# Layer 2's modulation computed as row sums on VectorE, and a longer gap between layer 1's gate matmuls and their transposes

## The chip, the cores and the metric

The kernel runs as one program on one core of a Trainium2 chip. The metric is the device time of one execution in microseconds (us). The engines are TensorE (PE in the profile; its weight loads are PEld), VectorE (DVE), ScalarE (ACT), GpSimd (POOL) and SyncE (SP), on whose queue all data transfers of this kernel are issued. Each engine works through its own instructions in order.

## The reference

A trunk of two layers over 512 tokens of width 1024 plus 256 context tokens. Per layer, shortened:

```python
shift, scale, gate = split(silu(c) @ ada_w + ada_b, 3)      # c: one vector of 1024; ada_w: 1024 x 3072
hx = rms_norm(x, norm_w) * (1 + scale) + shift              # the same for the context y, with c_ctx
... = split_cols(hx @ w_in)                                 # q, k, v, gates of three branches, merge gates
ret, na, gqa = retention(...), neighbourhood_attention(...), grouped_query_attention(...)
m = sum(sigmoid(mg_b) * (branch_b @ w_b_o) for the three branches)
x = x + gate * (m @ w_out)                                  # the same for y, in layer 1 only
return rms_norm(x, final_norm_w)                            # after layer 2
```

The change concerns the first line alone: `shift`, `scale` and `gate`, called the modulation here. For each layer it is a product of a 3072 x 1024 matrix with one vector (x) or two (x and context). Layer 1 is `l == 0` in the code, layer 2 is `l == 1`.

## The kernel before

Activations lie with features on the 128 partitions and tokens along the free dimension (8 tiles of 128 features; 768 columns in layer 1, 512 in layer 2's queries and outputs). Every large product is made of three matmuls (lines 286 to 288): weights are split into `whi` (cast by ScalarE, L270) and `wlo` (the remainder, by GpSimd or VectorE, L272), activations likewise. Weights come as a stream of 512 KB tiles `raw`, two buffers deep, issued on SP's queue in the order of use; `whi` and `wlo` have five half-tile buffers each.

The order of TensorE's instructions is the order in which the code is written (a manual schedule). On the other engines a scheduler places instructions by a simulated time and by priorities.

At the end of each layer stands `finish` (L1261), the end stage, in two parts:

- Eight merge units, one per feature tile d (`u_merge`, L1085): 24 matmuls of 512 columns and, in layer 1, 24 of 256 for the merge gate, then 12 and 12 for the retention branch's output projection. ScalarE takes the gate's PSUM bank through a tanh into the tile `mt`; VectorE multiplies the projection's bank into `mt` (L1114) and adds it to the sum `m[d]` (L1115). Then `m[d]` is split into a high part by ScalarE (L1278) and a low part by VectorE (L1279), in tiles `mhl` for d below 4 and `gat` above.
- The output projection `g_out` (L1289): two passes over the token columns (512 and 256 in layer 1, 256 and 256 in layer 2), eight tiles each, each a sum over all eight split tiles, that of d = 7 last. VectorE evicts a bank with the gate `cG` and the old x (`xo`) (L1302), ScalarE squares, VectorE sums the squares (L383). The norm of the first pass is computed under the second.

The modulation stands in slices of 256 of the 3072 columns (`ada_slice`, L345). A slice is a 1 MB transfer into `araw`; eight matmuls (L352) that write four groups of 32 PSUM rows; a copy of the bank by VectorE into `aev` (L355); two transposes by TensorE (L360), placed some microseconds of TensorE's work later by `defer`; and a few small VectorE instructions (L365 to L371) that leave `adaT`, `cA` (from the scale) and `cG` (from the gate). Layer 1's first eight slices run at the kernel's start. The other sixteen run in layer 1's end stage: two after each merge unit d = 0 to 3 (layer 1's four gate slices after d = 0 and 1, layer 2's shift and scale after that), one after each of d = 4 to 7, and layer 2's four gate slices in the first pass of `g_out`. After d = 7, `due(True)` forces the transposes of that slice at once.

Of the kernel before, what the change touches and what calls it, by code (L numbers as in the profile page):

```python
# [8 lines left out]
F32 = mybir.dt.float32  # L9
# [4 lines left out]
ALU = mybir.AluOpType  # L14
# [3 lines left out]
DEPTH = 2  # L18
# [18 lines left out]


@with_exitstack
def trunk_kernel(ctx: ExitStack, tc: tile.TileContext, xt, wcol, wv, adaw, wbr, wout, nabias, vecs,  # L40
                 cst, cst16, out, taps=None):
    nc = tc.nc

    def tap(name, ap, where):
# [205 lines left out]
    NKEEP = ((0.01, 0.01, 0.01, 0.0), (5.0, 0.01, 4.0, 0.0))  # L250
    GAP = 2.0
    XA0 = 5
    SN0 = 5
    LEAD = 1.5
    stream = []
# [81 lines left out]
    ap_wout = [[[wout[l, t] for t in range(8)] for _ in range(2)] for l in range(DEPTH)]  # L337


    def ada_load(l, s, apool, bufs):  # L340
        raw = apool.tile([128, KT, 256], F32, tag="araw", name="araw", bufs=bufs)
        nc.sync.dma_start(out=raw, in_=adaw[l, s].rearrange("p (k c) -> p k c", c=256))
        return raw

    def ada_slice(l, s, apool, bufs, raw=None):  # L345
# [739 lines left out]
    def u_merge(l, b, d, g, m, getpool):  # L1085
        gq = G_ALL if l == 0 else G_LAT
        nq = NT if l == 0 else NX
        src = [ap_wcol[l][CT_MG + 8 * b + d]]
        if d % 2 == 0:
            src.append(ap_wbr[l][b][d // 2])  # L1090

        def gen(ws):
            if d % 2 == 0:
                wbr_now[0] = ws[1]
            t = getpool().tile([128, nq], F32, tag="mt", name="mt", bufs=1)

            def ev(ps, o, n):
                nc.scalar.activation(t[:, o:o + n], ps, AF.Tanh, scale=0.5)
            yield from g_proj(ws[0], gq, ev)
            hi, lo = wbr_now[0][d % 2]  # L1100
            if len(g) < 4:
                due(True)
            for o, n in gq:
                ps = pbank()
                for k in range(4):
                    c = slice(k * 128, k * 128 + 128)
                    gh, gl = g[k]
                    mm3(ps[:, :n], hi[:, c], lo[:, c], gh[:, o:o + n], gl[:, o:o + n], k == 0, k == 3)
                    if k == 3:
                        c = slice(o, o + n)  # L1110
                        if b == BR_NA:
                            nc.vector.scalar_tensor_tensor(m[d][:, c], t[:, c], 1.0, ps[:, :n], op0=ALU.add, op1=ALU.mult)
                        else:
                            nc.vector.scalar_tensor_tensor(t[:, c], t[:, c], 1.0, ps[:, :n], op0=ALU.add, op1=ALU.mult)  # L1114
                            nc.vector.tensor_tensor(m[d][:, c], m[d][:, c], t[:, c], op=ALU.add)  # L1115
                    yield 3 * n * NS
        return Unit(nq * 36 * NS, src, gen)

# [142 lines left out]
    def finish(l, m, mtp):  # L1261
        nq = NT if l == 0 else NX
        cm = pool(f"wo{l}")
        op = cm.__enter__()
        mp = env["mp"]
        mhl = {}
        for d, u in enumerate(end_units[l]):
            run([u], True)
            if l == 0:
# [19 lines left out]
        def g_out(half, o, n):  # L1289
            for d in range(KT):  # L1290
                w = getw(ap_wout[l][half][d])
                xo = op.tile([128, 512], F32, tag="xo", name="xo", bufs=2)
                nc.sync.dma_start(out=xo[:, :n], in_=xsrc[:, d * st + o:d * st + o + n])
                ps = pbank()
                for k in range(KT):
# [3 lines left out]
                    if k == KT - 1:  # L1299
                        s = 1 if o >= NX else 0  # L1300
                        with tc.high_priority(HP):
                            nc.vector.scalar_tensor_tensor(xn[d][:, o:o + n], ps[:, :n], cG[l][:, d, s:s + 1], xo[:, :n],  # L1302
                                                           op0=ALU.mult, op1=ALU.add)
                            sumsq(accs["t"], xn[d], d == 0, slice(o, o + n), op)
                        if l == 0 and o == 0:
                            nc.sync.dma_start(out=env["xsave"][:, d * NX:(d + 1) * NX], in_=xn[d][:, :NX])
                        tap(f"x{l}", xn[d][:, o:o + n], (d, slice(None), slice(o, o + n)))
# [128 lines left out]
def _layout(x, c, ctx, c_ctx, ada_w, ada_b, norm_w, w_in, ret_log_decay, ret_gn_w, na_rpb,  # L1436
# [12 lines left out]
    a["adaw"] = aw[:, :, :, order].reshape(DEPTH, KT, 128, 12, 256).transpose(0, 3, 2, 1, 4).reshape(DEPTH, 12, 128, 2048)  # L1449
# [18 lines left out]
    return a  # L1468


_INS = ["xt", "wcol", "wv", "adaw", "wbr", "wout", "nabias", "vecs", "cst", "cst16"]


# [19 lines left out]
```

## Time and profile before

| | |
|---|---|
| median of 3 runs | 1732.67 us (1730.77 to 1734.23) |
| profiled execution, own time | 1732.19 us |
| its span, first to last instruction | 1730.4 us |
| mean granted TensorE clock | 0.993 |
| PE busy | 1660.4 us (96%) |
| DVE, ACT, POOL busy | 61%, 46%, 32% |
| layer 1's end stage | about 799 to 1000 us |
| layer 2's end stage | about 1590 us to the end |

Times in the trace are microseconds from the start of the span. A row of the timeline gives start, length, engine, line, operation, output and inputs, and in brackets how long the engine had been idle and what ended it. A row of a window gives its length, each engine's busy time with its instructions, the granted clock, the transfers' share and GB/s. Matmuls overlap in the records, so the distance between two starts, and not the length, is what a matmul costs.

### The profile page before, as it was taken

To read this page: it belongs to the slowest core of one execution; us is meant where nothing else is said; L and a number is where in the kernel's file an instruction comes from. 1 tells how busy PE (TensorE), PEld (TensorE's weight loads), DVE (VectorE), ACT (ScalarE), POOL (GpSimd) and SP (SyncE) were. 2 spreads that over 40 slices of the span, in tenths; PEclk is the share of its full clock that TensorE was granted. 3 is DMA by queue.
4 is the path that set the end of the run, shared out by engine and by line. 5 is a ranking of instruction groups with operands and counts; after the bars stand their busy time and mean duration, and the time that the engine had idled before them with its cause. 6 is when DMAs were issued, how large, how long until landed. Compare 5 with 4: busy or idle time off the path is not lost. (4 is left out here: it accounts for less than half of the span.)

```text
span 1730.4 us, 26113 instructions
## 1 busy us (share of the span) xinstructions
PE 1660.4 (96%) x9940; PEld 1438.0 (83%) x9940; DVE 1058.3 (61%) x2201; ACT 797.0 (46%) x1570; POOL 555.5 (32%) x486
## 2 busy tenths in 40 slices
PE   5999999999999999999999999999999999999996
PEld 4878888888899889888887889877787898888786
DVE  6666567666655665565324766668777646556456
ACT  4455564555553443443223445654555534444342
POOL 1423332332332222322222343433333333243432
PEclk9999999999999999999999999999999999999998
DMA  8211111111111111214536521311111222222344
GB/s 319 86 46 56 58 46 53 37 49 37 37 50 59 50 58 40 62 49 155 211 134 207 171 94 51 99 51 62 49 49 51 71 63 72 61 78 69 104 139 148
DMA packets 43053, 146.38 MB, mean 85 GB/s; under 512 B 4912, under 2 KB 10160, under 8 KB 39856
## 3 DMA queue, kind: packets, MB, share of 16 engines
q1 hardware_dynamic: 42928, 144.72, 25.2%
q8 instruction: 78, 1.28, 0.3%
q14 instruction: 47, 0.39, 0.1%
HBM read 140.51 MB, written 4.19 MB: 84 GB/s over the span
## 5 line engine op out<-in xcount | busy, mean ns | idle before, releaser
L272 POOL TENSOR_TENSOR wlo<-raw,whi 128x512 fp32r<-128x512 f32 x345 | 456.3, 1328 | 959.3 <-ACT whi L270 904.8
L286 PE MATMUL pj<-hxh,whi 128*128 128x512 f32 (+1 forms) x1192 | 429.4, 360 | 1.2 <-DVE mt L1114 1.0
L287 PE MATMUL pj<-hxl,whi 128*128 128x512 f32 (+1 forms) x1192 | 414.3, 348 | 0.0
L288 PE MATMUL pj<-hxh,wlo 128*128 128x512 f32 (+1 forms) x1192 | 414.2, 348 | 0.0
L270 ACT CAST whi<-raw 128x512 fp32r<-128x512 f32 x376 | 231.1, 618 | 282.1 <-PE pj L287 169.9
L288 PEld LDWEIGHTS pj<-hxh,wlo 128*128 128x128 f32 x1192 | 225.3, 189 | 30.4
L286 PEld LDWEIGHTS pj<-hxh,whi 128*128 128x128 f32 x1192 | 225.7, 189 | 20.3 <-DVE mt L1114 1.4
L287 PEld LDWEIGHTS pj<-hxl,whi 128*128 128x128 f32 x1192 | 226.2, 190 | 18.3
L447 DVE TENSOR_TENSOR pl<-pt,ph 128x512 fp32r<-128x512 f32 (+2 forms) x208 | 126.8, 626 | 53.9 <-ACT ph L446 51.9
L446 ACT CAST ph<-pt 128x512 fp32r<-128x512 f32 (+2 forms) x208 | 107.6, 533 | 70.5 <-PE pt L632 30.6
L286 PE MATMUL pj<-gat,whi 128*128 128x512 f32 (+1 forms) x320 | 112.2, 351 | 2.0 <-ACT gat L925 2.0
L287 PE MATMUL pj<-gat,whi 128*128 128x512 f32 (+1 forms) x320 | 110.2, 344 | 0.2 <-DVE gat L926 0.2
L288 PE MATMUL pj<-gat,wlo 128*128 128x512 f32 (+1 forms) x320 | 110.1, 344 | 0.0
L286 PE MATMUL pt<-hxh,whi 128*128 128x512 f32 (+1 forms) x256 | 96.3, 376 | 1.0 <-ACT hxh L411 1.0
L287 PE MATMUL pt<-hxl,whi 128*128 128x512 f32 (+1 forms) x256 | 95.1, 372 | 1.9 <-DVE hxl L412 1.9
L288 PE MATMUL pt<-hxh,wlo 128*128 128x512 f32 (+1 forms) x256 | 94.7, 370 | 0.0
L870 ACT ACTIVATE p<-p,nm,rq 128x768 f32<-128x768 f32 x64 | 65.4, 1024 | 46.7 <-DVE nm L868 46.1
L861 DVE TENSOR_SCALAR_CACHE_REDUCE p<-s 128x384 f32<-128x384 f32 x128 | 69.1, 555 | 27.0 <-PE s L860 25.6
L318 PE MATMUL pj<-whi,hxh 128*128 128x256 f32 x240 | 69.4, 289 | 0.0
L286 PEld LDWEIGHTS pj<-gat,whi 128*128 128x128 f32 x320 | 61.1, 191 | 9.2 <-ACT gat L925 2.5
L319 PE MATMUL pj<-wlo,hxh 128*128 128x256 f32 x240 | 68.5, 285 | 0.0
L320 PE MATMUL pj<-whi,hxl 128*128 128x256 f32 x240 | 68.5, 285 | 0.0
(304 smaller groups left out, 3529.8 us busy)
## 6 DMA issues: line engine op xcount, KB each, us to landing
raw<-in_wcol_dram SPq DMA_DIRECT2D x116, 512.0 KB, 3.5
araw<-in_adaw_dram SPq DMA_DIRECT2D x24, 1024.0 KB, 6.4
raw<-in_wout_dram SPq DMA_DIRECT2D x32, 512.0 KB, 3.5
raw<-in_wbr_dram SPq DMA_DIRECT2D x24, 512.0 KB, 3.5
raw<-in_wv_dram SPq DMA_DIRECT2D x16, 512.0 KB, 3.5
bias<-in_nabias_dram SPq DMA_DIRECT2D x16, 384.0 KB, 3.1
x<-in_xt_dram SPq DMA_DIRECT2D x8, 384.0 KB, 5.8
xo<-in_xt_dram SPq DMA_DIRECT2D x8, 256.0 KB, 3.6
```

What stands on the lines that cost most here:

```text
L270: nc.scalar.copy(hi, raw[:, c])
L272: lo_eng.tensor_tensor(lo, raw[:, c], f(hi), op=ALU.subtract)
L286: mm(ps, lhsT=sh, rhs=mh, start=start, stop=False)
L287: mm(ps, lhsT=sh, rhs=ml, start=False, stop=False)
L288: mm(ps, lhsT=sl, rhs=mh, start=False, stop=stop)
L318: mm(o, lhsT=sh[:, tok], rhs=hi, start=(k == 0), stop=False)
L319: mm(o, lhsT=sh[:, tok], rhs=lo, start=False, stop=False)
L320: mm(o, lhsT=sl[:, tok], rhs=hi, start=False, stop=(k == KT - 1))
L446: nc.scalar.copy(ph[:, :n], pt[:, :n])
L447: nc.vector.tensor_tensor(pl[:, :n], pt[:, :n], f(ph[:, :n]), op=ALU.subtract)
L861: nc.vector.tensor_scalar(P[:, jj, kk], s[:, :384], 1.0, -3.0e38, op0=ALU.mult, op1=ALU.max, accum_out=mx[:, i:i + 1])
L870: nc.scalar.activation(P[:, a], P[:, a], AF.Exp, bias=nm[:, a:a + 1], scale=rqe[:, 2 * hf + a:2 * hf + a + 1], accum_out=sm[:, a:a + 1])
```

## The change

Layer 2's twelve slices leave TensorE. A class `RowSums` computes the same numbers on VectorE: the weights of one output feature tile lie as 128 rows of 1024 (`adav`, a transposed layout prepared outside the kernel), the vector c is broadcast to all partitions (`ada_c`, one transfer from `cvec`, then tanh on ScalarE and one VectorE instruction per vector), and a multiply with a sum along the row (`tensor_tensor_reduce`, 128x512, two halves per row) gives a column of the modulation.

In layer 1's end stage 16 tiles with two vectors make 64 such row sums: three behind each of the 16 branch evictions of the merge units, two behind each of the eight evictions of `g_out`'s first pass. In layer 2's end stage 8 tiles with one vector make 16: two behind each merge eviction; these are layer 2's gates. The output that nobody reads goes to the tile just used (`mt` or `xo`), for which `mt` gets a second buffer and `xo` a third.

Layer 1's four gate slices stay on TensorE, one after each of d = 0 to 3 with one `araw` buffer, and their transposes are deferred by 5.0 instead of 2.0.

```diff
+            cb = self.cb = ap.tile([128, conds, D], F32, name="ada_c")
+            nc.sync.dma_start(out=cb, in_=cvec[0:conds * D].partition_broadcast(128).rearrange("p (s k) -> p s k", s=conds))
+            for s in range(conds):
+                th = ap.tile([128, D], F32, tag="avw", name="avw", bufs=bufs)
+                nc.scalar.activation(th, cb[:, s], AF.Tanh, scale=0.5)
+                nc.vector.scalar_tensor_tensor(cb[:, s], th, 1.0, cb[:, s], op0=ALU.add, op1=ALU.mult)
...
+        def load(self, i):
+            if i < len(self.tiles):
+                self.raws[i] = self.ap.tile([128, D], F32, tag="avw", name="avw", bufs=self.bufs)
+                nc.sync.dma_start(out=self.raws[i], in_=adav[self.tiles[i]])
...
+        def step(self, n, scratch):
+            for _ in range(min(n, len(self.todo))):
...
+                nc.vector.tensor_tensor_reduce(out=scratch[:, :H], in0=self.raws[i][:, H * h:H * h + H],
+                                               in1=self.cb[:, s, H * h:H * h + H], scale=1.0, scalar=0.0,
+                                               op0=ALU.mult, op1=ALU.add, accum_out=r[:, s, h:h + 1])
+                if (h, s) != (1, self.conds - 1):
+                    continue
+                self.load(i + self.bufs)
+                n_ = self.conds
+                nc.vector.tensor_tensor(r[:, :n_, 0:1], r[:, :n_, 0:1], r[:, :n_, 1:2], op=ALU.add)
+                dst = adaT[1][:, t, :n_]
+                nc.vector.tensor_scalar(dst, r[:, :n_, 0:1].rearrange("p s h -> p (s h)"), 0.5, vcol(1, V_ADAB, t),
+                                        op0=ALU.mult, op1=ALU.add)
...
-            t = getpool().tile([128, nq], F32, tag="mt", name="mt", bufs=1)
+            t = getpool().tile([128, nq], F32, tag="mt", name="mt", bufs=2)
...
+                        if b == BR_RET:
+                            env["sums"].step(STEPS[l] // len(gq), t)
...
+        env["sums"] = (RowSums(op, [t + 8 * i for t in range(8) for i in range(2)], 2, 3) if l == 0 else
+                       RowSums(op, list(range(16, 24)), 1, 2))
...
-                for i, s in (((0, 8), (0, 9)), ((0, 10), (0, 11)), ((1, 0), (1, 1)), ((1, 2), (1, 3)), ((1, 4),), ((1, 5),),
-                             ((1, 6),), ((1, 7),))[d]:
-                    defer(2.0, ada_slice(i, s, op, 2))
+            if l == 0 and d < 4:
+                defer(5.0, ada_slice(0, 8 + d, op, 1))
...
-                xo = op.tile([128, 512], F32, tag="xo", name="xo", bufs=2)
+                xo = op.tile([128, 512], F32, tag="xo", name="xo", bufs=3)
...
+                            env["sums"].step(2, xo)
...
-                if l == 0 and half == 0 and i in (16, 28, 40, 52):
-                    defer(2.0, ada_slice(1, 8 + (i - 16) // 12, op, 2))
```

The lines of the changed kernel lie one (up to L337) to about fifty further down. Its row sums appear as ISA, each followed by a short instruction that writes the sum.

VectorE, around the end of layer 1's first merge unit, before; `mhl` is the low part of m[0], `aev` the copies of the two slices' banks:

```order
L1114 SCALAR_TENSOR_TENSOR mt<-mt,pj 128x256
L1115 TENSOR_TENSOR m<-m,mt 128x256
L355 COPY aev<-pt 128x256
L1279 TENSOR_TENSOR mhl<-m,mhl 128x768
L355 COPY aev<-pt 128x256
L365 TENSOR_REDUCE ada_red<-pt 128x4 x2
```

The same place in the changed kernel; `ada_c` is the vector c on all partitions, `avw` a tile of the transposed weights:

```order
L1163 SCALAR_TENSOR_TENSOR mt<-mt,pj 128x256
L1164 TENSOR_TENSOR m<-m,mt 128x256
L354 SCALAR_TENSOR_TENSOR ada_c<-avw,ada_c 128x1024 x2
L1330 TENSOR_TENSOR mhl<-m,mhl 128x768
L373 ISA mt,ada_sum<-avw,ada_c 128x512
L373 ISA ada_sum 128x1
L373 ISA mt,ada_sum<-avw,ada_c 128x512
L373 ISA ada_sum 128x1
L404 COPY aev<-pt 128x256
```

The copy that the slice's transposes wait for now stands behind the two instructions on `ada_c`, the low part of m[0] and two row sums.

VectorE, at the end of layer 1's last merge unit, before; the last `gat` is the low part of m[7], the row after that but one the first eviction of `g_out`:

```order
L1114 SCALAR_TENSOR_TENSOR mt<-mt,pt 128x512
L1115 TENSOR_TENSOR m<-m,mt 128x512
L1279 TENSOR_TENSOR gat<-m,gat 128x768
L1114 SCALAR_TENSOR_TENSOR mt<-mt,pj 128x256
L355 COPY aev<-pt 128x256
L1115 TENSOR_TENSOR m<-m,mt 128x256
L365 TENSOR_REDUCE ada_red<-pt 128x4
L367 TENSOR_TENSOR adaT_101<-ada_red,vec 128x2x2
L371 TENSOR_SCALAR cA_103<-adaT_101,vec 128x2
L1279 TENSOR_TENSOR gat<-m,gat 128x768
```

The same place in the changed kernel, from the eviction of the second part of d = 7 on:

```order
L1163 SCALAR_TENSOR_TENSOR mt<-mt,pj 128x256
L373 ISA mt,ada_sum<-avw,ada_c 128x512
L373 ISA ada_sum 128x1
L1164 TENSOR_TENSOR m<-m,mt 128x256
L380 TENSOR_TENSOR ada_sum<-ada_sum 128x2
L373 ISA mt,ada_sum<-avw,ada_c 128x512
L373 ISA ada_sum 128x1
L273 TENSOR_TENSOR wlo<-raw,whi 128x512
L382 TENSOR_SCALAR adaT_101<-ada_sum,vec 128x2
L373 ISA mt,ada_sum<-avw,ada_c 128x512
L373 ISA ada_sum 128x1
L1330 TENSOR_TENSOR gat<-m,gat 128x768
```

Three row sums, a weight remainder (`wlo`) and two small instructions now stand between that eviction and the low part of m[7], and one more row sum stands ahead of the eviction.

SP's queue, where layer 1's end stage begins, before:

```order
L263 DMA raw<-in_wbr_dram 128x1024
L263 DMA raw<-in_wcol_dram 128x1024 x2
L342 DMA araw<-in_adaw_dram 128x2048 x4
L263 DMA raw<-in_wbr_dram 128x1024
L263 DMA raw<-in_wcol_dram 128x1024
```

And in the changed kernel:

```order
L264 DMA raw<-in_wbr_dram 128x1024
L264 DMA raw<-in_wcol_dram 128x1024 x2
L350 DMA ada_c<-in_cvec_dram 128x2048
L391 DMA araw<-in_adaw_dram 128x2048
L364 DMA avw<-in_adav_dram 128x1024 x3
L391 DMA araw<-in_adaw_dram 128x2048
L364 DMA avw<-in_adav_dram 128x1024
L264 DMA raw<-in_wbr_dram 128x1024
```

The next weights (`raw` of `wbr`) now stand behind the broadcast and the fourth `avw`, whose buffer is free once the first tile's four row sums are done.

## Rows read from the trace of the kernel before

**Rows 1.** The page's first part: busy us, share, instructions.

```profile
PE 1660.4 (96%) x9940; PEld 1438.0 (83%) x9940; DVE 1058.3 (61%) x2201; ACT 797.0 (46%) x1570; POOL 555.5 (32%) x486
```

**Rows 2.** Windows of units d=1, d=5: us; PE, PEld, DVE, ACT, POOL busy.

```profile
811.86:826.96 15.10, 15.10 (x110) 12.46 (x108) 5.85 (x14) 3.58 (x6) 3.86 (x4) 1.00 0.68 248
872.30:886.30 14.00, 14.00 (x92) 11.72 (x90) 4.28 (x10) 3.58 (x6) 4.05 (x3) 1.00 0.39 128
```

**Rows 3.** Timeline of PE around one slice in the first output pass.

```profile
927.54 0.39 PE L287 MATMUL pt<-mhl,whi 128*128 128x512 f32 x1
927.77 0.39 PE L288 MATMUL pt<-mhl,wlo 128*128 128x512 f32 x1
929.09 0.50 PE L286 MATMUL pt<-mhl,whi 128*128 128x512 f32 x1
929.43 0.40 PE L287 MATMUL pt<-mhl,whi 128*128 128x512 f32 x1
...
931.06 0.39 PE L288 MATMUL pt<-mhl,wlo 128*128 128x512 f32 x1
931.43 0.48 PE L286 MATMUL pt<-gat,whi 128*128 128x512 f32 x1
931.75 0.40 PE L287 MATMUL pt<-gat,whi 128*128 128x512 f32 x1
```

**Rows 4.** Timeline of PE at the end of the last merge unit.

```profile
914.15 0.28 PE L288 MATMUL pj<-gat,wlo 128*128 128x256 f32 x1
...
916.13 0.41 PE L360 MATMUL pt<-ident,aev 128*128 128x128 f32 x2 [0.70 <-DVE aev L355]
916.30 0.48 PE L286 MATMUL pt<-mhl,whi 128*128 128x512 f32 x1
```

**Rows 5.** A group of DVE at L606: busy us, mean ns, idle before.

```profile
L606 DVE CUSTOM_DVE_ANT_1 pb<-s,bias 128x512 f32<-128x512 f32 x32 | 21.9, 687 | 6.6 <-PE s L604 6.2
```

**Rows 6.** Timeline of DVE after merge unit d=0, then PE there.

```profile
812.81 1.44 DVE L1115 TENSOR_TENSOR m<-m,mt 128x256 f32<-128x256 f32 x1
814.17 0.41 DVE L355 COPY aev<-pt 128x256 f32<-128x256 f32 x1
815.15 0.96 DVE L1279 TENSOR_TENSOR mhl<-m,mhl 128x768 fp32r<-128x768 f32 x1 [0.57 <-ACT mhl L1278]
...
811.95 1.93 PE L352 MATMUL pt<-araw,cst_c 128*32 128x256 f32 x32
```

**Rows 7.** Timeline of SP there, and the landing times of the araw transfers.

```profile
805.20 9.07 SPq L342 DMA_DIRECT2D araw<-in_adaw_dram  x4
814.37 0.38 SPq L263 DMA_DIRECT2D raw<-in_wbr_dram  x1
...
DMA to landing us min/median/max: 4.7/6.4/19.6
```

**Rows 8.** Timeline of DVE at the end of the last merge unit, then POOL.

```profile
913.04 0.69 DVE L1114 SCALAR_TENSOR_TENSOR mt<-mt,pt 128x512 f32<-128x512 f32 x1 [1.47 <-PE pt L288]
913.76 0.69 DVE L1115 TENSOR_TENSOR m<-m,mt 128x512 f32<-128x512 f32 x1
914.37 0.95 DVE L1279 TENSOR_TENSOR gat<-m,gat 128x768 fp32r<-128x768 f32 x1
...
915.05 1.40 POOL L272 TENSOR_TENSOR wlo<-raw,whi 128x512 fp32r<-128x512 f32 x1 [4.29 <-ACT whi L270]
```

**Rows 9.** The same end in layer 2: DVE, then PE.

```profile
1663.56 0.69 DVE L1114 SCALAR_TENSOR_TENSOR mt<-mt,pj 128x512 f32<-128x512 f32 x1 [0.54 <-PE pj L288]
1664.28 1.60 DVE L1115 TENSOR_TENSOR m<-m,mt 128x512 f32<-128x512 f32 x1
1666.57 0.69 DVE L1279 TENSOR_TENSOR gat<-m,gat 128x512 fp32r<-128x512 f32 x1
...
1666.59 0.39 PE L286 MATMUL pt<-gat,whi 128*128 128x256 f32 x1 [0.55 <-ACT gat L1278]
1667.31 0.38 PE L287 MATMUL pt<-gat,whi 128*128 128x256 f32 x1 [0.34 <-DVE gat L1279]
```

More of the change, by code (lines that the diff above doesn't have):

```diff
@@ L39, in trunk_kernel @@
 @with_exitstack
-def trunk_kernel(ctx: ExitStack, tc: tile.TileContext, xt, wcol, wv, adaw, wbr, wout, nabias, vecs,
-                 cst, cst16, out, taps=None):
+def trunk_kernel(ctx: ExitStack, tc: tile.TileContext, xt, wcol, wv, adaw, adav, wbr, wout, nabias, vecs,
+                 cvec, cst, cst16, out, taps=None):
     nc = tc.nc
@@ L252, in trunk_kernel @@
     XA0 = 5
+    STEPS = (6, 2)
     SN0 = 5
@@ L337, in trunk_kernel, with __init__ @@
     ap_wout = [[[wout[l, t] for t in range(8)] for _ in range(2)] for l in range(DEPTH)]
+    class RowSums:
+        def __init__(self, ap, tiles, conds, bufs):
+            self.ap, self.bufs = ap, bufs
+            self.H = H = D // 2
+            cb = self.cb = ap.tile([128, conds, D], F32, name="ada_c")
[4 more added lines that the diff above has]
+                nc.vector.scalar_tensor_tensor(cb[:, s], th, 1.0, cb[:, s], op0=ALU.add, op1=ALU.mult)
+            self.raws, self.red = {}, {}
+            self.tiles, self.conds = tiles, conds
+            self.todo = [(i, h, s) for i in range(len(tiles)) for h in range(2) for s in range(conds)]
+            for i in range(bufs):
+                self.load(i)
+        def load(self, i):
[4 more added lines that the diff above has]
+            for _ in range(min(n, len(self.todo))):
+                i, h, s = self.todo.pop(0)
+                t, H = self.tiles[i], self.H
+                if (h, s) == (0, 0):
+                    self.red[i] = cp.tile([128, 2, 2], F32, tag="ada_sum", name="ada_sum", bufs=2)
+                r = self.red[i]
+                nc.vector.tensor_tensor_reduce(out=scratch[:, :H], in0=self.raws[i][:, H * h:H * h + H],
[9 more added lines that the diff above has]
+                                        op0=ALU.mult, op1=ALU.add)
+                if t >= 16:
+                    nc.vector.tensor_scalar(cG[1][:, t - 16, :n_], dst, 0.25, None, op0=ALU.mult)
+                elif t >= 8:
+                    nc.vector.tensor_scalar(cA[1][:, t - 8, :], dst, 1.0, vcol(1, V_NW, t - 8), op0=ALU.add, op1=ALU.mult)
@@ L340, in ada_load @@
     def ada_load(l, s, apool, bufs):
         raw = apool.tile([128, KT, 256], F32, tag="araw", name="araw", bufs=bufs)
-        nc.sync.dma_start(out=raw, in_=adaw[l, s].rearrange("p (k c) -> p k c", c=256))
+        nc.sync.dma_start(out=raw, in_=adaw[s].rearrange("p (k c) -> p k c", c=256))
         return raw
@@ L1268, in finish @@
             run([u], True)
-            if l == 0:
-                for i, s in (((0, 8), (0, 9)), ((0, 10), (0, 11)), ((1, 0), (1, 1)), ((1, 2), (1, 3)), ((1, 4),), ((1, 5),),
-                             ((1, 6),), ((1, 7),))[d]:
-                    defer(2.0, ada_slice(i, s, op, 2))
+            if l == 0 and d < 4:
+                defer(5.0, ada_slice(0, 8 + d, op, 1))
             tap(f"m{l}", m[d][:, :nq], (d, slice(None), slice(0, nq)))
@@ L1304, in g_out @@
                             sumsq(accs["t"], xn[d], d == 0, slice(o, o + n), op)
+                        if l == 0 and o == 0:
+                            env["sums"].step(2, xo)
                         if l == 0 and o == 0:
@@ L1448, in _layout @@
     order = [t for s in range(8) for t in (s, 8 + s)] + list(range(16, 24))
-    a["adaw"] = aw[:, :, :, order].reshape(DEPTH, KT, 128, 12, 256).transpose(0, 3, 2, 1, 4).reshape(DEPTH, 12, 128, 2048)
+    a["adaw"] = aw[0][:, :, order].reshape(KT, 128, 12, 256).transpose(2, 1, 0, 3).reshape(12, 128, 2048)
+    a["adav"] = aw[1].transpose(2, 3, 0, 1).reshape(24, 128, D)
+    a["cvec"] = np.concatenate([c[0], c_ctx]).reshape(2 * D)
     br = np.stack([g(w_ret_o), g(w_na_o), g(w_gqa_o)], axis=1)
@@ L1468, in _layout @@
     return a
-_INS = ["xt", "wcol", "wv", "adaw", "wbr", "wout", "nabias", "vecs", "cst", "cst16"]
+_INS = ["xt", "wcol", "wv", "adaw", "adav", "wbr", "wout", "nabias", "vecs", "cvec", "cst", "cst16"]
 def kernel(**inputs):
```

## The prediction

> **What bounds the kernel now.** I read the busy shares first: TensorE is busy 1660.4 of 1730.4 us, VectorE 61% of the span [rows 1]. Such an average says little of one stage, so I took windows of the end stage next. In the merge units of layer 1 TensorE has no gap at all (15.10 us busy of 15.10, 14.00 of 14.00) at a granted clock of 1.00, VectorE works 5.85 and 4.28 us of these, ScalarE 3.58, GpSimd about 4 [rows 2]. There a microsecond taken from TensorE is a microsecond of the kernel, and VectorE has 9 to 10 us free per unit. Last I read the timeline for what a slice costs TensorE, and which VectorE instruction TensorE waits for nearest.
>
> **What goes.** Matmuls of 512 columns start 0.23 us apart (927.54 to 927.77). With a slice between, the next one starts 1.32 us later (927.77 to 929.09), and the one after that 0.34 instead of 0.23 later: the eight matmuls cost 1.32 - 0.23 + 0.11 = 1.20 us. The two transposes cost 0.37 - 0.23 (931.06 to 931.43) plus 0.32 - 0.23 behind them, 0.23 us [rows 3]. A slice alone is thus 1.43 us. A unit with two slices takes 1.10 us more than one with one [rows 2], so a pair is 2.53. The slice after d = 7 has its transposes at once, and TensorE waits 0.70 us for the copy: 914.15 to 916.30 is 2.15 us, less 0.12 for the last matmul of 256 columns, plus 0.09 behind it, 2.12 us [rows 4].
>
> Before, layer 1's end stage holds four pairs, seven single slices and that last one: 4 x 2.53 + 7 x 1.43 + 2.12 = 22.2 us. After, four single slices stay: 4 x 1.43 = 5.7. **TensorE loses 16.5 us.**
>
> **What comes.** No row sum exists in the trace, but the same kind of instruction does, with a maximum in place of a sum: 0.69 us for 128x512 [rows 5]. In the changed order each row sum writes the scratch that the one before wrote, so I count them as dependent; dependent instructions of 0.69 us start 0.72 apart (913.04 to 913.76) [rows 8]. Six per merge unit are 4.3 us, the small instructions of 1.5 tiles some 0.9 us. With the 4.3 us of a one-slice unit VectorE reaches about 9.5 of the 12.6 us that a unit takes without a slice (14.00 - 1.43). In the first output pass a tile takes 24 x 0.227 = 5.4 us of TensorE, and VectorE needs there an eviction, the squares' sum and a weight remainder of about 0.7 to 0.9 us each, two row sums and small ones: 4.3 us. So the row sums as such lie beside TensorE's work and I charge nothing for them. The two tanh of 128x1024 lie in ScalarE's 9 idle us per unit. If that cover fails, the price is the second rival's below.
>
> What costs is order: at three places VectorE does row sums ahead of something that TensorE waits for next.
>
> *(a) After d = 0.* The second update of m[0] ended at 812.81 + 1.44 = 814.25. Then come the two instructions on `ada_c`: 0.69 us for 512 columns and 0.96 for 768 make about 1.23 for 1024, 2.45 together, to 816.7. The low part of m[0], 0.96, ends 817.65; two row sums 819.1; the copy, 0.41, at 819.55. TensorE has the slice's matmuls at 811.95 [rows 6], goes on at 813.15, and reaches the transposes after the 24 matmuls of the 512 columns, at 818.6. It waits 1.0 us. Behind the transposes TensorE's whole queue waits. Bounds: 0, if the copy comes in time, and 2.5, if one GpSimd subtraction (1.40 [rows 8]) holds a row sum. I take 1.0. For d = 1 to 3 the copy stands behind one row sum only and the transposes 5 us away: nothing.
>
> *(b) At the end of layer 1's merge units.* Set T = 914.27, TensorE's last merge matmul. The low part of m[6] runs until T + 1.05 [rows 8]. Behind it stand a row sum, the eviction, a row sum, the update, a small one, a row sum, a weight remainder, a small one, a row sum, and then the low part of m[7]: 4 x 0.72 + 0.45 + 0.45 + 0.72 + 2 x 0.2 + 0.96 = 5.9, so T + 6.9. TensorE, with no slice in between, starts the output pass at T and needs that tile for its 23rd matmul, T + 5.0. Wait 1.9; with the GpSimd subtraction of this place, which starts at T + 0.78, ahead of the first row sum, 3.0. Bounds 1.0 and 4.2 (two such collisions); I take 2.5. Before, this end cost 2.12 us in another way, and that is already counted as gone.
>
> *(c) The same end in layer 2.* TensorE already waits there: the matmul at 1667.31 for the low part that started at 1666.57 [rows 9]. Two row sums now stand ahead of that: 1.45 us, and a little for the short instructions, 1.6. Bounds 0.8, where the update that took 1.60 under GpSimd is shorter, and 3.2, where a row sum is held. I take 1.6.
>
> Elsewhere: at the end of the first output pass the row sum fits in the time in which ScalarE squares, nothing. The transfers' bytes hardly change (12 MB of weights as before, 1.5 MB of vectors more). On SP the next weights stand behind the fourth `avw`, which waits for the first tile's four row sums, about 821 instead of 814.4 [rows 7]; they serve the second half of unit d = 2, about 833, and need a transfer and two casts until then: hidden, with some 5 us to spare. Later loads have a unit or more.
>
> Sum: 16.5 - 1.0 - 2.5 - 1.6 = 11.4 us. From the profiled execution's 1732.2 that is 1720.8; the median shown is 0.5 above it, so I say **1721.3 us**. Its own range, by the bounds of a to c (1.8 to 9.9 us lost, the far end needing all at once) and the scatter of the runs, is 1716.5 to 1726.
>
> **The rivals.** *First: the waits don't come.* VectorE's independent instructions overlap a little in the trace (L1279 starts 0.61 after an instruction of 0.69 [rows 8]), and m[7] or the copies may come in time. For it: slack of a few tenths decides at each place. Against it: three places at once, and in layer 2 TensorE waits already. With a and b nearly gone and c at its lower end the loss is 1, the time 1717; with none, 1716.
>
> *Second: row sums and GpSimd shut each other out.* The update of 128x256 at 812.81 took 1.44 us, that of 128x512 at 1664.28 took 1.60 [rows 6, 9] against 0.69 of the free one at 913.76 [rows 8]; these read two tiles in SBUF, as a row sum will. The maximum of rows 5 has one input in PSUM, so its 0.69 says nothing of that. If every GpSimd instruction of a unit (4.05 us [rows 2]) holds a row sum, VectorE needs 9.5 + 4 = 13.5 of 12.6 us; over d = 4 to 7 it falls 3.5 us behind, which adds to b, and a and c go to their upper ends (1.5 and 1.6 more): 11.4 - 6.6 = 4.8 us gained, 1728. Against it: VectorE waits for TensorE anyway in each unit, and not each subtraction meets a row sum. The Trainium skill has this as a rule ("SBUF — State Buffer", section "Who interferes with whom"): a VectorE instruction with two SBUF inputs and a GpSimd instruction that reads SBUF exclude each other for a whole instruction, and issue order decides who waits. The long updates above agree with it; by the rule each collision costs up to a whole GpSimd instruction, which is what this rival adds up.
>
> *Third, on the other side: the broadcast comes late.* `ada_c` is one 1 MB transfer that reads the same 8 KB 128 times; none like it is in the trace. VectorE's queue stands behind it, with the slice's copy, the next evictions and, through the `avw` loads, SP's weights. It can be issued at 805.2 and must be there about 812 for the first tanh. The 1 MB transfers land after 6.4 us at the median, 19.6 at most [rows 7]. Past 812 each microsecond goes straight to wait a; from 11.4 us on the kernel is slower. At 19.6 it is there at 824.8, 12.8 late: 1734. For it: nothing measured; against it: the like transfers of this stage took no longer than TensorE's slice at 811.95 could bear.
>
> **How the numbers follow.** Forecast 0.64, first rival 0.15, second 0.14, third 0.07. The range 1715 to 1729 takes in the forecast, the first and most of the second rival, and leaves out the third and the far end of the second, under 0.15. No change means within 0.2%, 3.5 us of 1732.7, so above 1729.2 there is no gain to be told. Faster: 0.64 + 0.15 + 0.05 of the second; same: 0.09, the rest of the second; slower 0.07.
>
> **What will show it.** Right: no matmuls of layer 2's slices near 870 to 960; merge units d = 5 to 7 about 12.6 us long; waits of TensorE on `aev` at d = 0, on the low part of `gat` at both ends, of 1, 2.5 and 1.6 us; row sums of 0.7 us, dependent ones 0.72 apart. Wrong would be: units longer than 12.7 us or row sums that average over 1 us (second rival); VectorE idle on `ada_c` after 814 (third); TensorE waiting for weights after the first unit, which would be the queue on SP that I have hidden.

## The result and the profile after

The changed kernel takes 1724.5 us (median of 5 runs, 1720.7 to 1726.4) beside 1732.5 for the one before: ratio 0.9948, 95% interval 0.9937 to 0.9959, so 7 to 11 us less. Forecast were 1721.3 us and 11.4 us less, with a range of 1715 to 1729. The direction and the range held. Of 16.5 us that TensorE no longer works, about half arrived.

The profiled execution took 1724.5 us (span 1722.7, mean granted clock 0.991). Its busy line answers to [rows 1]: TensorE 11 us less, VectorE 73 us more.

```profile
PE 1649.4 (96%) x9724; PEld 1432.6 (83%) x9724; DVE 1131.0 (66%) x2380; ACT 799.2 (46%) x1573; POOL 557.9 (32%) x486
```

To see where time went I took the start of the same matmul in both traces at the borders of the stages. A column is the length of a stage in us, the last line what I had forecast for the difference.

| | merge units, layer 1 | first output pass | second pass to layer 2's first attention matmul (L652 after) | from there to layer 2's output stage | its first two tiles | rest |
|---|---|---|---|---|---|---|
| before | 116.96 | 49.67 | 65.69 | 631.70 | 7.17 | 52.07 |
| after | 106.51 | 47.25 | 68.45 | 634.20 | 9.84 | 49.27 |
| difference | -10.45 | -2.42 | +2.76 | +2.50 | +2.67 | -2.80 |
| forecast | -10.8 + 1.0 (a) | -5.7 + 2.5 (b) | 0 | 0 | +1.6 (c) | 0 |

*Merge units.* The window of unit d = 6 of the changed kernel, which like every unit from d = 5 on has no slice, to be read as [rows 2]:

```profile
881.50:894.03 12.53, 12.53 (x75) 11.08 (x73) 8.59 (x23) 3.58 (x6) 4.23 (x3) 1.00 0.46 148
```

A unit takes 12.5 us without a gap in TensorE, as forecast (12.6). VectorE is busy 8.6 of it instead of 4.3 in the one-slice unit of [rows 2]: the row sums lie beside the matmuls.

*Place a.* VectorE after unit d = 0, then TensorE, answering to [rows 6]:

```profile
818.02 0.68 DVE L373 CUSTOM_DVE_ANT_0 mt<-avw,ada_c 128x512 f32<-128x512 f32 x1
818.74 0.69 DVE L373 CUSTOM_DVE_ANT_0 mt<-avw,ada_c 128x512 f32<-128x512 f32 x1
819.36 0.42 DVE L404 COPY aev<-pt 128x256 f32<-128x256 f32 x1
...
813.02 1.07 PE L401 MATMUL pt<-araw,cst_c 128*32 128x256 f32 x16 [0.30 <-DMA araw<-in_adaw_dram]
...
819.36 0.39 PE L289 MATMUL pt<-hxh,wlo 128*128 128x512 f32 x1
819.84 0.44 PE L409 MATMUL pt<-ident,aev 128*128 128x128 f32 x2
```

The copy ends at 819.78, where I had put 819.55. But TensorE came 1.0 us later than I had put it: this unit began 0.69 later in this execution, and the slice waited 0.30 for its own weights. The transposes' turn, one matmul's distance of 0.23 behind 819.36, was thus 819.59; they start at 819.84, right behind the copy. The wait is 0.25 us instead of 1.0. These two row sums took 0.68 and 0.69 and started 0.72 apart, the figure used.

*Place b.* VectorE at the end of the merge units, GpSimd and TensorE beside it, answering to [rows 8]; then the window behind the wait:

```profile
907.51 1.78 DVE L373 CUSTOM_DVE_ANT_0 mt<-avw,ada_c 128x512 f32<-128x512 f32 x1
909.23 0.41 DVE L1163 SCALAR_TENSOR_TENSOR mt<-mt,pj 128x256 f32<-128x256 f32 x1
...
911.92 0.68 DVE L373 CUSTOM_DVE_ANT_0 mt<-avw,ada_c 128x512 f32<-128x512 f32 x1
912.53 0.95 DVE L1330 TENSOR_TENSOR gat<-m,gat 128x768 fp32r<-128x768 f32 x1
...
907.33 1.42 POOL L273 TENSOR_TENSOR wlo<-raw,whi 128x512 fp32r<-128x512 f32 x1 [4.29 <-ACT whi L271]
...
913.53 0.50 PE L288 MATMUL pt<-gat,whi 128*128 128x512 f32 x1 [1.53 <-DVE gat L1330]
...
915.27 0.63 PE L287 MATMUL pj<-mhl,whi 128*128 128x512 f32 x1
915.70 0.63 PE L288 MATMUL pj<-mhl,whi 128*128 128x512 f32 x1
```

```profile
913.50:917.80 4.30, 4.26 (x12) 3.38 (x13) 4.09 (x9) 1.25 (x2) 1.28 (x1) 0.60 0.57 180
```

The low part of m[7] ended at T + 6.9 (T = 906.55, TensorE's start of the output pass; end 913.48), as forecast, and the matmul that needs it started 1.8 us later than its turn; 0.2 us more went just before, for the high part. What I had not counted stands behind it: after the wait the granted clock is 0.60 in this stretch, that is mostly the lower of its two levels, 1.2 GHz, and matmuls start 0.43 us apart instead of 0.23. That cost another 1.7 us, together 3.7 (47.25 us for this pass beside 43.55 in the experiment that removes the wait).

*Place c.* The same end in layer 2, VectorE and TensorE, answering to [rows 9], then the window behind:

```profile
1657.37 1.60 DVE L1164 TENSOR_TENSOR m<-m,mt 128x512 f32<-128x512 f32 x1
1659.00 0.69 DVE L373 CUSTOM_DVE_ANT_0 mt<-avw,ada_c 128x512 f32<-128x512 f32 x1
...
1660.22 0.69 DVE L373 CUSTOM_DVE_ANT_0 mt<-avw,ada_c 128x512 f32<-128x512 f32 x1
1660.83 0.69 DVE L1330 TENSOR_TENSOR gat<-m,gat 128x512 fp32r<-128x512 f32 x1
...
1659.67 0.38 PE L287 MATMUL pt<-gat,whi 128*128 128x256 f32 x1 [0.56 <-ACT gat L1329]
1661.58 0.48 PE L288 MATMUL pt<-gat,whi 128*128 128x256 f32 x1 [1.52 <-DVE gat L1330]
```

```profile
1661.50:1665.60 4.10, 4.02 (x21) 4.02 (x22) 1.19 (x6) 1.65 (x3) 1.28 (x1) 0.58 0.43 153
```

The wait grew from 0.34 to 1.52, and again a stretch at the lower clock followed: 2.7 us instead of 1.6.

*The second output pass.* The largest loss was not in the forecast. It is followed through four queues; first the kernel before (VectorE, SP, ScalarE), then the changed one.

```profile
969.05 0.47 DVE L1302 SCALAR_TENSOR_TENSOR m<-pt,cG,xo 128x256 f32<-128x256 f32 x1
...
974.99 0.68 DVE L272 TENSOR_TENSOR wlo<-raw,whi 128x512 fp32r<-128x512 f32 x1
...
975.73 0.33 SPq L263 DMA_DIRECT2D raw<-in_wout_dram  x1
...
976.50 0.62 ACT L270 CAST whi<-raw 128x512 fp32r<-128x512 f32 x1 [1.69 <-PE pt L287]
977.02 0.72 ACT L411 ACTIVATE hxh<-ny,adaT 128x512 fp32r<-128x512 f32 x1
...
990.42 0.62 ACT L270 CAST whi<-raw 128x512 fp32r<-128x512 f32 x1 [0.73 <-DMA raw<-in_wv_dram]
```

```profile
954.79 1.58 DVE L373 CUSTOM_DVE_ANT_0 xo<-avw,ada_c 128x512 f32<-128x512 f32 x1
...
957.50 0.68 DVE L373 CUSTOM_DVE_ANT_0 xo<-avw,ada_c 128x512 f32<-128x512 f32 x1
...
958.11 0.47 DVE L1353 SCALAR_TENSOR_TENSOR m<-pt,cG,xo 128x256 f32<-128x256 f32 x1
...
963.64 0.68 DVE L273 TENSOR_TENSOR wlo<-raw,whi 128x512 fp32r<-128x512 f32 x1
...
964.38 0.33 SPq L264 DMA_DIRECT2D raw<-in_wout_dram  x1
...
965.67 0.62 ACT L271 CAST whi<-raw 128x512 fp32r<-128x512 f32 x1 [2.77 <-DMA raw<-in_wout_dram]
966.20 0.72 ACT L460 ACTIVATE hxh<-ny,adaT 128x512 fp32r<-128x512 f32 x1
...
981.35 0.62 ACT L271 CAST whi<-raw 128x512 fp32r<-128x512 f32 x1 [2.69 <-PE pt L288]
...
982.93 0.68 DVE L432 TENSOR_TENSOR acc<-acc,sq 128x256 f32<-128x256 f32 x1 [1.36 <-ACT sq L431]
...
985.35 0.50 PE L288 MATMUL pt<-hxl,whi 128*128 128x512 f32 x1 [2.21 <-DVE hxl L461]
```

Counted from TensorE's start of that pass (965.97 before, 953.80 after), the pass's first eviction comes at +4.3 instead of +3.1, because two row sums, one of them 1.58 us long, stand ahead of it. VectorE's weight remainders (`wlo`) slip with it: one ends at +10.5 instead of +9.7. Each frees a `raw` buffer, and SP issues the next weights 0.06 us behind it, at +10.6 instead of +9.8. Their cast on ScalarE moves from +10.5 to +11.9, and the first `hxh` of layer 2 stands behind that cast: +12.4 instead of +11.05.

The same happens again further down, and there it reaches TensorE. The first `wv` weights are issued at +22.1 instead of +21.0 and take 5.3 us to land instead of 3.4; their cast starts at +27.5 instead of +24.5. Behind it in ScalarE's queue stands a square, for which VectorE's sum `acc` waits 1.36 us, and behind that sum stands the last `hxl`, for which TensorE waits 2.2 us. Slow clock follows.

*The two other columns* (+2.50 and -2.80) have the same instructions in both kernels; the last section says what they are.

### The profile page after: what moved, and what is told of

Read it like the earlier page. It is cut to its first block, busy times and chain, and to the rows that moved or that the text cites. A ratio compares the mean times of both kernels' runs of the same rounds, so it can differ in the third digit from the quotient of the medians.

```text
span 1722.7 us, 25888 instructions
## 1 busy us (share of the span) xinstructions
PE 1649.4 (96%) x9724; PEld 1432.6 (83%) x9724; DVE 1131.0 (66%) x2380; ACT 799.2 (46%) x1573; POOL 557.9 (32%) x486
## 5 line engine op out<-in xcount | busy, mean ns | idle before, releaser
L919 ACT ACTIVATE p<-p,nm,rq 128x768 f32<-128x768 f32 x64 | 65.4, 1024 | 47.1 <-DVE nm L917 46.5
```

Source lines behind the costliest of these rows:

```text
L919: nc.scalar.activation(P[:, a], P[:, a], AF.Exp, bias=nm[:, a:a + 1], scale=rqe[:, 2 * hf + a:2 * hf + a + 1], accum_out=sm[:, a:a + 1])
```

## Experiments

The theory is that row sums cost nothing but order: they stand ahead of an instruction that TensorE waits for, at b, c and the second pass, and such a wait brings slow clock with it. The rivals are that VectorE has too much to do, with GpSimd holding its row sums, or that TensorE's early arrival alone makes these waits. In brackets stand the ratio to the kernel before and its 95% interval; the changed kernel has 0.9948 (0.9937 to 0.9959).

**Layer 1's last merge unit without row sums** (ratio 0.9914, 0.9901 to 0.9926)

```diff
-    STEPS = (6, 2)
+    STEPS = ([3, 3, 3, 3, 4, 4, 4, 0], [2, 2, 2, 2, 2, 2, 2, 2])
...
-                            env["sums"].step(STEPS[l] // len(gq), t)
+                            env["sums"].step(STEPS[l][d], t)
```

> The six row sums of layer 1's last merge unit move to units d = 4 to 6 (4 behind each eviction there instead of 3, none at d = 7); all 64 are done. Theory (order, then clock): TensorE's 1.53 us wait for the low part of m[7] at the end of the merge units goes, and with it the ten matmuls that follow it at 0.43 instead of 0.23 us (1.9 us); the profile shows TensorE at clock 1.00 there, and the time falls by 3.0 to 3.7 us, to about 1721. Rival (VectorE simply has too much to do, held by GpSimd): the row sums only get late earlier, units d = 4 to 6 stretch beyond 12.6 us or the wait stays at 1 us or more, and the time stays at 1724 to 1725.

The wait is gone and the clock stays up, in the two windows from the start of the output pass on:

```profile
907.35:912.80 5.45, 5.45 (x26) 4.51 (x25) 4.00 (x6) 1.98 (x3) 1.42 (x1) 1.00 0.11 41
912.80:918.20 5.40, 5.40 (x25) 4.49 (x24) 3.72 (x6) 1.88 (x3) 1.30 (x1) 1.00 0.59 193
```

The first pass takes 43.55 us instead of 47.25, and units d = 4 to 7 the same 50.4, though d = 4 to 6 now hold eight row sums each. The 3.7 us of place b are order. The median is 6 us lower; the part over 3.7 is in stages that this edit does not touch.

**The last two tiles of the first output pass without row sums** (0.9933, 0.9921 to 0.9945)

```diff
+    GSTEPS = [3, 3, 3, 3, 2, 2, 0, 0]
...
-                            env["sums"].step(2, xo)
+                            env["sums"].step(GSTEPS[d], xo)
```

> The 16 row sums of the first output pass stand behind its first six tiles (3, 3, 3, 3, 2, 2) and none behind the last two. Theory: VectorE enters the second pass about 1.5 us earlier relative to TensorE, and in the second pass VectorE is the one that is behind; the 2.2 us wait of TensorE for hxl at about 985 falls below 1 us and the loss of 2.8 us between 960 and 997 falls to under 1, time about 1722.5. Rival: the wait at hxl is set by TensorE's own earlier arrival (VectorE has the same chain of evictions, norms and remainders as before and TensorE gained there), then the wait stays within 0.4 us of 2.2 and the time at 1724.5.

The stage from the second pass to layer 2's attention takes 66.05 us instead of 68.45, and the first wait at `hxl` is 0.66. Over all kernels of this study that compute the row sums as they stood there, it takes 66.87 to 68.89 (seven profiles), and 66.05 to 66.35 in the four that have that place free and the remainders as before. The rival of TensorE's early arrival falls. That the row sums cause the loss is thus shown by the stage; the total (median 1722.8) is not told apart from the changed kernel's.

The way is read from the traces. In every kernel whose second pass has remainders on VectorE, each weight load of this pass but the last is issued 0.06 to 0.07 us after one of them ends. Which of the two late casts counts is seen in the kernel of the first experiment, where the row sums of the first pass stand as in the changed one (ScalarE, TensorE; its pass began at 950.89):

```profile
977.67 0.62 ACT L271 CAST whi<-raw 128x512 fp32r<-128x512 f32 x1 [2.32 <-DMA raw<-in_wv_dram]
...
981.68 0.50 PE L288 MATMUL pt<-hxl,whi 128*128 128x512 f32 x1 [2.15 <-DVE hxl L461]
```

Its first `hxh` comes early, at +11.5, and yet TensorE waits 2.15. In six of the seven profiles that wait ends 4.1 us after the first `wv` weights landed, and in all seven the later the landing (+25.4 to +28.0), the longer the stage. In the four with the place free these weights are issued at +21.1 to +21.4 and take 3.5 to 3.6 us; in the seven they are issued at +21.6 to +22.8 and take 3.5 to 5.3. The later issue is the remainders' doing; why most of the later loads also took longer, no run here shows.

**Layer 2's last two merge units without row sums** (0.9935, 0.9921 to 0.9949)

```diff
-    STEPS = (6, 2)
+    STEPS = ([3, 3, 3, 3, 3, 3, 3, 3], [3, 3, 3, 3, 2, 2, 0, 0])
...
-                            env["sums"].step(STEPS[l] // len(gq), t)
+                            env["sums"].step(STEPS[l][d], t)
```

> Layer 2's 16 row sums stand behind units d = 0 to 5 (3, 3, 3, 3, 2, 2) and none behind d = 6 and 7. Theory: the wait for the low part of m[7] in layer 2 goes back from 1.52 to about the 0.3 us of the kernel before, and the slow clock behind it (1.4 us) goes; time lower by 1.2 to 2.7 us, 1722 to 1723. Rival (the 1.60 us update under GpSimd sets it, not the row sums): the wait stays above 1 us and the time within 0.5 us.

```profile
1657.04 0.39 PE L287 MATMUL pt<-gat,whi 128*128 128x256 f32 x1 [0.56 <-ACT gat L1329]
1657.77 0.39 PE L288 MATMUL pt<-gat,whi 128*128 128x256 f32 x1 [0.34 <-DVE gat L1330]
```

The waits are those of the kernel before to the hundredth [rows 9], and the first two tiles take 7.17 us instead of 9.84. In this profile place b, whose code is untouched, had its wait of 1.53 without slow clock: the first pass took 45.65 us. The wait alone is thus 2.1 us there (45.65 - 43.55), and the slow stretch comes in some executions only. The total (median 1722.5) is not told apart from the changed kernel's.

**All three** (0.9905, 0.989 to 0.992; median 1717.0 us)

```diff
-    STEPS = (6, 2)
+    GSTEPS = [2, 2, 2, 2, 2, 0, 0, 0]
+    STEPS = ([3, 4, 4, 4, 4, 4, 4, 0], [3, 3, 3, 3, 2, 2, 0, 0])
...
-                            env["sums"].step(STEPS[l] // len(gq), t)
+                            env["sums"].step(STEPS[l][d], t)
...
-                            env["sums"].step(2, xo)
+                            env["sums"].step(GSTEPS[d], xo)
```

> All three at once: layer 1's merge units 3, 4, 4, 4, 4, 4, 4, 0 behind each eviction pair's two halves counted per eviction, the first output pass 2 each behind its first five tiles, layer 2 as 3, 3, 3, 3, 2, 2, 0, 0. If the three places are independent, as the order theory has it, the gains add: 3.5 + 2 + 2 = about 7.5 us, time about 1717. If VectorE's total work is the limit, the time stays above 1722, and units d = 1 to 3 stretch or their slice's copies come late.

Stage by stage the gains add: the first pass takes 43.55 us, the stage from the second pass to layer 2's attention 66.35, layer 2's first two tiles 7.17. The time is 1717.0 us against 1717 expected, 7.5 less than the changed kernel; the three medians taken singly would make 9.7, and that difference is within what the executions of one kernel scatter. Merge units and first pass take 106.49 and 43.55 us, 16.6 less than before, which is what I had worked out for TensorE's work (16.5). TensorE's first wait for `hxl` is 0.96. This is the version that beats both kernels.

**No row sums at all** (0.9930, 0.9918 to 0.9943)

```diff
-                nc.vector.tensor_tensor_reduce(out=scratch[:, :H], in0=self.raws[i][:, H * h:H * h + H],
...
+                nc.vector.tensor_copy(r[:, s, h:h + 1], self.raws[i][:, H * h:H * h + 1])
```

> The 80 row sums are left out (a copy of one column stands in for each, so layer 2's modulation is not computed); loads, broadcast, tanh and the small instructions stay. Theory: the row sums cost only through their order at three places, so that this kernel is no faster than the one that moves them away from these places: ratio to the kernel before 0.989 to 0.992, about 1716 to 1718, TensorE without waits for gat at both ends and the wait at hxl below 1 us. Rival (the row sums as such load VectorE and, through the time in which GpSimd holds them, the path): 1713 or less.

The total missed the expectation: with a median of 1721.4 it is 4 us slower than with all row sums done at the right places. Layer 1's merge units take 112.74 us instead of 106.5, because TensorE waited behind unit d = 1 for a slice's weights (SP, then TensorE), and slow clock followed:

```profile
806.44 16.95 SPq L364 DMA_DIRECT2D avw<-in_adav_dram  x6
823.50 0.37 SPq L389 DMA_DIRECT2D araw<-in_adaw_dram  x1
...
830.91 1.93 PE L399 MATMUL pt<-araw,cst_c 128*32 128x256 f32 x16 [4.17 <-DMA araw<-in_adaw_dram]
```

With nobody holding the `avw` buffers, six of their loads went out ahead of the slice's weights, which SP issued at 823.5 instead of 817.7. The row sums had been pacing the queue. Stage by stage the theory holds: units d = 4 to 7 take 50.41 us, the first pass 43.55, the second to layer 2's attention 66.29, layer 2's tiles 7.17, each within 0.1 us of the kernel with moved row sums. In those places a row sum costs nothing.

**The transposes deferred by 2.0 again** (0.9963, 0.9950 to 0.9976)

```diff
-                defer(5.0, ada_slice(0, 8 + d, op, 1))
+                defer(2.0, ada_slice(0, 8 + d, op, 1))
```

> Layer 1's gate transposes are deferred by 2.0 again instead of 5.0; all else as in the changed kernel. Theory: the copies of the slices' banks come as late as now (819.8, 832.8, 844.6, 858.1), TensorE wants them at 816.8, 831.0, 845.0 and 858.9: waits of 3.0 and 1.8 us in units 1 and 2, with a stretch of slow clock behind one or both (1.7 us each), none in units 3 and 4; time 1729 to 1732, most of the gain gone. Rival: the scheduler puts the copies ahead of the row sums again, or the first wait is short; then within 1.5 us of 1724.5 and the deferral is worth nothing.

```profile
820.83 0.44 PE L409 MATMUL pt<-ident,aev 128*128 128x128 f32 x2 [2.69 <-DVE aev L404]
```

The first wait came as expected (2.7 of 3.0), the second hardly (0.35 of 1.8), since the first had moved TensorE back; no slow clock followed here. The merge units take 109.93 us instead of 106.51. The median, 1727.2, is 2.6 us longer and below the 1729 to 1732 expected, and the intervals overlap. So the deferral covers place a and is worth 3.4 us in its stage, less than I expected; the total does not show it for certain.

**TensorE kept at work during the waits** (0.9926, 0.9915 to 0.9938)

```diff
-                ps = pbank()
+                ps = nxt.pop() if nxt else pbank()
...
+                    if half == 0 and d == 0 and k == KT - 1:
+                        nxt.append(pbank())
+                        for _ in range(8 if l == 0 else 16):
+                            mm(nxt[0][:, :n], lhsT=wk(w, 0)[0], rhs=mhl[0][0][:, o:o + n], start=True, stop=True)
```

> Where TensorE waits for m[7] at the ends of both layers' merge units, it does 8 matmuls of 512 columns (layer 1) and 16 of 256 (layer 2), 1.8 us each time, into a bank that the next tile overwrites. The work thus takes the place of the wait. Theory (the slow stretch behind the wait comes from TensorE's idling): the waits shrink to under 0.6 us, no stretch at clock 0.5 follows either of them, the units behind start as early as with the wait alone, and the time falls by the slow stretches, 1.7 us each where they fell: 1721 to 1723. Rival (the clock falls there for another reason, as load): the slow stretches stay, time 1724.5 or more.

```profile
910.00 1.98 PE L1354 MATMUL pj<-mhl,whi 128*128 128x512 f32 x8
...
912.03 0.39 PE L288 MATMUL pt<-gat,whi 128*128 128x512 f32 x1
```

```profile
914.20:917.80 3.60, 3.60 (x18) 2.98 (x17) 3.53 (x8) 1.15 (x2) 0.37 (x1) 1.00 0.71 226
1657.00:1661.00 4.00, 4.00 (x35) 4.00 (x35) 2.58 (x5) 1.86 (x4) 1.40 (x1) 1.00 0.58 165
```

Superfluous work makes the kernel 3.8 us faster (the intervals just touch). The first pass takes 45.36 us, that is 43.55 and the 1.8 of the added matmuls, and the clock stays at 1.00 at both places. The same wait of 1.5 us, left idle, was followed by slow clock in three of four profiles at place b and five of five at c; one of 1.32 us at b, in the kernel with the remainders on VectorE below, was not. So it is the idling that brings the slow stretch, as far as one profile with the wait filled can show it.

**The share of d = 7 behind the second tile's first seven** (0.9926, 0.9915 to 0.9938)

```diff
+            held = []
+
+            def part(k, d, w, ps, xo):
...
+                    if k == KT - 1 and half == 0 and d == 0:
+                        held.append((d, w, ps, xo))
+                        break
+                    if k == KT - 1 and held:
+                        part(KT - 1, *held.pop())
+                        yield 3 * n * NS
+                    part(k, d, w, ps, xo)
```

> The row sums stand as in the changed kernel; in the output projection's first pass the share of d = 7 of the first tile is done only after the second tile's first seven, in both layers. TensorE then needs m[7] 4.8 us later in layer 1 and 2.4 us later in layer 2. Theory: both waits go (1.5 and 1.5 + 0.56 us) with the slow stretches behind them, 3.6 + 2.7 us, and time falls to 1718 to 1720, more than by moving row sums at these two places, since layer 2's older wait of 0.9 goes too. Rival: the first two tiles' evictions come close together and VectorE with its row sums falls behind them, which gives 1 to 2 us back in the third tile; 1721 to 1723.

Both waits went without a row sum moved; the first pass takes 43.55 us. The median, 1720.8, lies between the two expectations. In layer 2 what was won was given back, as the rival had it: TensorE waited 0.85 us for a weight remainder, which only the two kernels with this order show, and 3.53 for the norm of the first half (the kernel before has such a wait too), and from the output stage to the end it took 59.69 us instead of 59.11. With both edits, the moved row sums and this order:

> The row sums moved away from all three places, and the share of d = 7 of the first output tile behind the second tile's first seven, in both layers. In layer 1 no wait is left at this place, so nothing changes there (time from the first output tile to the second pass 43.5 us). In layer 2 the older wait of 0.56 and 0.34 goes. Theory: 0.9 us less than with the moved row sums alone, about 1716. Rival: the two evictions that now come together push VectorE, ScalarE or a weight remainder back in layer 2's short tiles (2.9 us), and the gain is given back before the end: 1717 or more.

Measured: 0.9916 (0.9894 to 0.9937), median 1718.3, the first pass 43.55, the waits of 0.85 and 3.52 there again. The rival's figure, but the interval does not part it from the moved row sums alone.

**Weight remainders of the first pass all on VectorE** (0.9939, 0.9921 to 0.9957)

```diff
-                lo_eng = nc.vector if i == 1 and env.get("lo_dve") else nc.gpsimd
+                lo_eng = nc.vector if env.get("lo_dve") and (i == 1 or env.get("lo_all")) else nc.gpsimd
...
+            env["lo_all"] = l == 0 and half == 0
```

> In layer 1's first output pass the weight remainders that GpSimd makes go to VectorE (8 or so, about 0.69 us each there); the row sums stand as in the changed kernel. Theory: a row sum that starts while a GpSimd subtraction runs is held until that ends; without any, every row sum of this pass takes about 0.69 us instead of the 1.57 of the first one behind each eviction, VectorE's busy time per tile falls by 0.2 us in spite of the added work, and the time stays within 2 us of the changed kernel's, since VectorE is not the bound there. Rival: the first row sum is long for another reason (the eviction before it, or the tile that its output goes to); then the 1.57 stay.

A tile of the changed kernel (GpSimd, VectorE), and one of this kernel, where GpSimd is idle until 948:

```profile
938.20 1.30 POOL L273 TENSOR_TENSOR wlo<-raw,whi 128x512 fp32r<-128x512 f32 x1 [4.14 <-ACT whi L271]
...
938.47 1.57 DVE L373 CUSTOM_DVE_ANT_0 xo<-avw,ada_c 128x512 f32<-128x512 f32 x1
```

```profile
937.80 0.68 DVE L373 CUSTOM_DVE_ANT_0 xo<-avw,ada_c 128x512 f32<-128x512 f32 x1
...
948.20 1.62 DVE L373 CUSTOM_DVE_ANT_0 xo<-avw,ada_c 128x512 f32<-128x512 f32 x1
...
947.99 1.29 POOL L273 TENSOR_TENSOR wlo<-raw,whi 128x512 fp32r<-128x512 f32 x1 [50.58 <-ACT whi L271]
```

The thirteen row sums of this pass beside which GpSimd is idle take 0.68 to 0.69; the first that meets it again takes 1.62. The time (median 1722.6) does not tell the two kernels apart. The mutual holding is real, and no loss of time from it shows here.

**Second pass's remainders all on GpSimd, on top of the moved row sums** (0.9914, 0.9889 to 0.9940)

```diff
+            env["lo_dve"] = FD[l] and not (l == 0 and half == 1)
```

> The row sums moved away from all three places, and in layer 1's second output pass all weight remainders on GpSimd (8 more there, 1.3 us each, 8 of 0.69 us less on VectorE). Theory: VectorE is what the start of layer 2 waits for; with 5 us less for it in this pass the waits at hxl (0.96, 0.73) fall below 0.4 us and the slow stretch behind them shortens, time 1 to 3 us lower than with the moved row sums alone, 1714 to 1716. Rival: the added GpSimd instructions hold VectorE as long as they relieve it, or TensorE waits for wlo; 1717 or more.

The stage to layer 2's attention takes 65.57 us instead of 66.35, without slow clock in this profile; the wait for `hxl` that was to fall below 0.4 is 1.03, and one of 0.42 for `wlo` is new. The times (median 1717.8) don't tell it from the kernel it builds on. Inconclusive as to the total.

## Why the prediction came out as it did

- **What goes (16.5 us): right.** With the waits removed, merge units and first pass are 10.5 + 6.1 = 16.6 us shorter.
- **Row sums beside TensorE's work cost nothing: right** in the merge units and the first pass; with all of them left out, the stages at these places were no shorter than with the row sums moved. They took 0.68 us where GpSimd did not hold them, 0.72 apart.
- **(a) 1.0 us: 0.25.** With 2.0 of deferral it was 2.7. The mechanism was right; the copy came 0.23 us later than put, TensorE 1.0.
- **(b) 2.5 us: 3.7.** One collision with GpSimd came (1.78 us at 907.51), independent instructions started closer than counted (909.56 after 909.23, 910.50 after 910.17), and the low part ended at T + 6.9, the value without either; the wait was 2.0 to 2.1. What the term lacked is the slow clock behind a wait, 1.6 to 1.7. That the low part came at the value without a collision, though one came, is luck: 1.1 us lost and 1.1 gained. The slow clock was to be seen before, in a window of the kernel before right behind TensorE's wait of 3.56 us for `rstd`, which ends at 1701.9:

```profile
1702.60:1708.00 5.40, 5.40 (x31) 5.40 (x31) 4.39 (x9) 1.77 (x4) 1.96 (x2) 0.59 0.81 256
```

  The Trainium skill ("TensorE: Matmul & The Clock Gate", section "HAM oscillation — how this bites in real kernels") describes a kernel whose TensorE waits for transfers between its groups of matmuls and finds its clock down after each wait. Those waits are longer than the 1.5 us here; the filled wait agrees on the cause, with 1.00 in place of 0.60.
- **(c) 1.6 us: 2.7,** for the same reason: 1.2 of added wait, and 1.5 of slow clock that the term did not have.
- **"At the end of the first output pass the row sum fits ..., nothing": wrong,** and the largest miss. It cost 2.1 us in the changed kernel's profile (68.45 against 66.35). I had looked at the row sum beside the squares alone. The row sums there push back VectorE's own weight remainders; these free the `raw` buffers for which SP's queue waits, and ScalarE's queue holds squares and norm behind the cast of the weights that come late.
- **SP's queue after the fourth `avw`: right,** TensorE had no wait for `raw` in the units. The broadcast (third rival) landed 4.5 us after its issue at 805.9, before the 812 that it had to meet.
- **Second rival: its mechanism exists, its price does not.** 18 of the 80 row sums took 1.39 to 1.80 us, each of them begun while a GpSimd subtraction ran; the other 62 took 0.67 to 0.75. That is the rule of the Trainium skill that the prediction named ("SBUF — State Buffer", section "Who interferes with whom"), and the trace agrees. But VectorE had the time.
- **The sum.** Forecast -11.4, between the profiles -7.7. By the table's columns the merge units did 0.6 better, the first pass 0.8 and layer 2's tiles 1.1 worse, the second pass 2.8 worse; +2.5 and -2.8 stand where the code is the same, which is scatter (below). The range held although a stage priced at nothing lost 2.8 us; that the two columns of scatter nearly cancel is luck.

## What to carry to other kernels

Work moved to an idle engine is free as throughput and is paid for as order: list, for each place where the bound engine changes its source of data, what now stands ahead of that source, and follow buffers and DMA queues too, not only the engine. Put the added work behind the first units of a stage and none behind the last. Price a wait of the matmul engine at its length plus a slow stretch: here that followed 8 of 9 waits of 1.5 us.

## What the runs showed of the hardware

- Slow clock is scatter too. In all 13 profiles TensorE waits about 2.05 us at the start of layer 2's end stage, on the same instructions; in 8 of them a stretch at 1.2 GHz follows, in 5 none. The like holds near 1220 us (9 of 13). Each such stretch costs 1.7 us (one minus the granted clock, summed over its length), and some cost two or three times that. Two profiles can thus differ by 3 us in stages that nothing touched. From layer 2's first attention matmul to its output stage, the four profiles with neither stretch take 631.6 to 631.9 us, the one with one 633.1, the eight with both 633.6 to 635.3. The changed kernel's profile has both, that of before neither; this is behind the +2.50 of the table. That of before has instead a stretch of twice the cost near 1700 us, which the changed one lacks; this is behind the -2.80.
- A faster consumer can slow the kernel: row sums that held their buffers kept a queue in the right order (4.2 us of wait without them).
